# Cross-attention's query projection in seven products, with eight products of the first rows in the lead

## The chip, the cores and the metric

The kernel runs on one core of a Trainium2 chip. The metric is the device time of one execution in microseconds; the time of a kernel is the median of its runs. Engines are named as in the profile: PE is TensorE, DVE is VectorE, ACT is ScalarE, POOL is GpSimd, and SP is the engine on whose queue nearly all transfers are issued.

## What is computed

One layer of a decoder trunk in float32, with 1024 tokens and a model width of 1024. It has three sub-layers, each with an RMSNorm before and after: token mixing (attention and a state-space mixer), cross-attention into 256 memory tokens, and a gated feed-forward of hidden width 2816. The parts that matter here, with `S = D = 1024`:

```python
x = x + rms_norm(merged @ w_mix_out, g_post_mix)
h = rms_norm(x, g_pre_xa)
q = (h @ w_xq).reshape(bsz, seq, XA_HEADS, XA_HEAD_DIM)     # 4 heads of 256
...                                                         # k, v of the memory, softmax, o
x = x + rms_norm(o @ w_xo, g_post_xa)
h = rms_norm(x, g_pre_ffn)
gate, up = _split(h @ w_gu, (FFN_HIDDEN, FFN_HIDDEN))
x = x + rms_norm((silu(gate) * up) @ w_down, g_post_ffn)
```

## The kernel before

**Products.** A float32 operand is split into a rounded part `hi` (type fp32r) and a rest `lo`; a product is then three matmuls, hi·hi, hi·lo and lo·hi (`mm3`, lines 103 to 107). `hi_sb` makes the first part (line 94 on POOL, 98 on ACT) and `lo_of` the second (line 101, on DVE unless another engine is given).

**Seven products.** A 2x2 block product can be had with seven block products instead of eight (Winograd's form of Strassen's method). `winograd_weights` (line 174) forms the four combinations of weight blocks on POOL (lines 183 to 186), and splits seven blocks. `winograd_pair` (line 222) runs the seven products, 12 matmuls of 512 columns each (`acc3`, lines 211 to 218). The activation side needs seven blocks as well: `b11`, `b21`, `b22` as they are, and `t1` to `t4`, which are differences. `b11` and `b21` hold the first 512 tokens ("first rows"), the other five need the second 512 too. The feed-forward uses this form from its column block 2 on (`strassen`, line 1654, blocks 2 to 21).

**The two output projections** (`out_proj`, line 1421) go over eight chunks of 128 tokens, four for each half. A chunk multiplies 8 row blocks of a weight held in SBUF (`big_weight`, line 1352), takes the post-norm from the accumulator (square on ACT, line 1437; `rstd_of` on POOL; scaling on DVE, line 1439; addition, line 1440), stores the new x by SP's queue (line 1441), and calls `pre_norm` (line 157), which scales again (line 161), transposes eight tiles on PE (line 165) and splits them. Two accumulators (`p2`) alternate, so a chunk's matmuls wait for the scaling of the chunk before the last.

**Query projection** (lines 1501 to 1510). For each of eight column blocks `f` and each half of the tokens, `proj` (line 1466) runs 8 row blocks x 3 matmuls. Blocks 0 and 1 of the first half run under the norm of the last chunk. The other weights come by SP into the tiles `x4` and are split by `wq_load` (line 1457).

**Scores and mixing** (lines 1522 to 1570). `soft` makes the scores of a chunk for four heads in one `p2` accumulator, and the softmax; `turn_` transposes, `mix` multiplies with v. Then come `w_xo` (line 1574) and the second `out_proj`.

**Feed-forward's start** (lines 1596 to 1651). Column blocks 0 and 1 (`NSTD = 2`) are done in the standard form, four projections of 24 matmuls each for a block. Beside them `combos` (line 1631) adds hi and lo together again (`whole`, line 1624) and makes `t1`, `t3`, `t2`, and a last loop makes `t4`.

**Order and room.** The instructions of each engine are put in order ahead of time by a scheduler that runs its own timing model; `behind(marks)` ties what a block issues behind given instructions on the same engine. Tiles live in pools that open and close like stacks from the left and the right end of SBUF; a tile in a room that another tile had waits for the last use of that one. `wmix` lies in `wbigA` on the right, `w_xo` in `wbigB`; the tiles of the query and, later, of the feed-forward take the same rooms.

## Time and profile before

| | |
|---|---|
| median of 3 runs | 2554.08 us (2549.73 to 2554.72) |
| profiled execution | 2557.14 us, span 2555.3 us |
| mean granted TensorE clock | 0.994 |
| busy in the span | PE 97%, DVE 70%, ACT 44%, POOL 33% |
| PE instructions | 12378 |
| output projection and query projection | 1542 to 1728 us of the span |
| scores and mixing, second output projection | 1728 to 1885 us |
| feed-forward up to the down projection | 1885 to 2318 us |

A row of the timeline gives start, duration, engine, line and form, and in brackets the idle time just before it and what ended it. PE's durations overlap: a matmul begins before the one ahead of it has ended. A row of the stages gives for a stretch of the span each engine's busy time with its number of instructions, then the granted clock, the busy share of the transfer engines and GB/s.

### The profile page before, as it was taken

What the parts mean: (1) busy time and instruction counts of PE and PEld (TensorE: products, weight loads), DVE (VectorE), ACT (ScalarE), POOL (GpSimd) and SP (SyncE); (2) the same over time, 40 slices, a digit from 0 to 9 for tenths busy, and PEclk for the clock granted to TensorE, in tenths of its full rate; (3) what the DMA queues carried; (4) which work ended last, traced back from release to release, by engine and by line L of the source; (5) the groups of instructions that cost most, each with busy time, mean ns of one, the idle gap of its engine ahead of it and who ended that gap; (6) DMA issues with size and microseconds to landing.
All of it is one profiled execution on the core that took longest, in us unless ns stands there. A gap on an engine that the chain in (4) does not pass through costs nothing. (4 is left out here: it accounts for less than half of the span.)

```text
span 2555.3 us, 33384 instructions
## 1 busy us (share of the span) xinstructions
PE 2472.5 (97%) x12378; PEld 2030.5 (79%) x12378; DVE 1790.9 (70%) x2093; ACT 1133.7 (44%) x2023; POOL 852.2 (33%) x650
## 2 busy tenths in 40 slices
PE   7999999999999999999999999999999999999998
PEld 5788888888778778777787778887787888888877
DVE  7765877766678787698898664316458667666997
ACT  5333555555556565565554203215233333334342
POOL 3221644443211111256565140101113233223762
PEclk9999999999999999999999999999999999999999
DMA  7431443333443433365332652311231322324232
GB/s 246 157 124 58 138 133 103 107 112 109 127 108 99 114 99 99 105 209 166 106 107 61 226 194 84 116 49 34 99 123 59 95 80 75 99 84 164 99 132 99
DMA packets 255275, 293.51 MB, mean 115 GB/s; under 512 B 17023, under 2 KB 175240, under 8 KB 254986
## 3 DMA queue, kind: packets, MB, share of 16 engines
q1 hardware_dynamic: 255114, 291.40, 36.7%
q8 instruction: 97, 1.59, 0.3%
q14 instruction: 64, 0.52, 0.1%
HBM read 200.10 MB, written 74.45 MB: 107 GB/s over the span
## 5 line engine op out<-in xcount | busy, mean ns | idle before, releaser
L898 DVE TENSOR_TENSOR_SCAN n<-n,mask 128x128 f32<-128x128 f32 (+7 forms) x128 | 187.7, 1492 | 24.7 <-ACT n L897 23.4
L101 DVE TENSOR_TENSOR sw<-sf,sw 128x512 fp32r<-128x512 f32 x150 | 121.0, 819 | 82.1 <-ACT sw L98 80.6
L915 ACT ACTIVATE wth<-tr,mone 128x512 fp32r<-128x512 f32 x192 | 110.6, 585 | 83.9 <-PE tr L912 81.8
L98 ACT ACTIVATE sw<-sf 128x512 fp32r<-128x512 f32 x150 | 92.0, 626 | 112.7 <-PE mm L217 97.2
L183 POOL TENSOR_TENSOR sf<-wr,wr 128x512 f32<-128x512 f32 x38 | 58.4, 1536 | 234.0 <-DMA wr<-in_w_gu_dram 150.1
L916 DVE SCALAR_TENSOR_TENSOR wtl<-tr,wth 128x512 fp32r<-128x512 f32 x192 | 99.6, 543 | 50.8 <-ACT wth L915 50.7
L98 ACT ACTIVATE sw<-wr 128x512 fp32r<-128x512 f32 x113 | 71.2, 631 | 125.7 <-PE mm L217 124.2
L217 PE MATMUL mm<-h,sw 128*128 128x512 f32 x320 | 124.8, 391 | 1.8 <-DVE sw L101 1.8
L215 PE MATMUL mm<-h,sw 128*128 128x512 f32 x320 | 122.6, 391 | 2.9 <-ACT h L98 2.3
L216 PE MATMUL mm<-h,sw 128*128 128x512 f32 x320 | 125.1, 391 | 0.0
L101 DVE TENSOR_TENSOR sw<-wr,sw 128x512 fp32r<-128x512 f32 x113 | 108.4, 961 | 19.8 <-ACT sw L98 19.7
L680 DVE SCALAR_TENSOR_TENSOR b<-b,prmT,b 128x1023 f32<-128x1023 f32 (+2 forms) x72 | 109.6, 1522 | 16.9 <-ACT b L674 16.3
L94 POOL TENSOR_SCALAR v<-va 128x512 fp32r<-128x512 f32 x16 | 20.6, 1290 | 286.2 <-PE av L925 165.3
L897 ACT ACTIVATE n<-sc 128x512 f32<-128x512 f32 (+1 forms) x192 | 88.7, 494 | 46.8 <-PE tr L912 28.8
L152 POOL TENSOR_SCALAR rstd<-ms 128x1 f32<-128x1 f32 x74 | 29.1, 393 | 240.2 <-ACT x L1437 113.4
L104 PE MATMUL mm<-oth,bw 128*128 128x512 f32 x256 | 104.0, 406 | 2.6 <-DVE a L1237 2.3
L104 PE MATMUL p<-bw,h 128*128 128x512 f32 x256 | 99.6, 394 | 3.3 <-DVE x L1439 2.4
L105 PE MATMUL mm<-otl,bw 128*128 128x512 f32 x256 | 100.8, 394 | 0.0
L106 PE MATMUL mm<-oth,bw 128*128 128x512 f32 x256 | 100.7, 393 | 0.0
L106 PE MATMUL p<-bw,h 128*128 128x512 f32 x256 | 100.6, 394 | 0.0
L105 PE MATMUL p<-bw,h 128*128 128x512 f32 x256 | 100.5, 393 | 0.0
L912 PE MATMUL tr<-ident,n 128*128 128x128 f32 x576 | 95.2, 274 | 3.3 <-DVE wtl L916 3.3
(616 smaller groups left out, 8010.9 us busy)
## 6 DMA issues: line engine op xcount, KB each, us to landing
wr<-in_w_gu_dram SPq DMA_DIRECT2D x80, 256.0 KB
wr<-in_w_in_dram SPq DMA_DIRECT2D x36, 512.0 KB
zr<-in_w_in_dram SPq DMA_DIRECT2D x28, 512.0 KB
gu_d<-t SPq DMA_DIRECT2D x44, 256.0 KB
wraw<-in_w_in_dram SPq DMA_DIRECT2D x20, 512.0 KB
zs_d<-zo SPq DMA_DIRECT2D x32, 256.0 KB
xs_d<-b SPq DMA_DIRECT2D x32, 256.0 KB
kl<-gt SPq DMA_DIRECT2D x64, 128.0 KB
```

The source lines that it names most:

```text
L98: A.activation(o, i, AF.Copy)
L101: eng.tensor_tensor(o, i, hi.bitcast(F32), ALU.subtract)
L104: first = T.matmul(ps, sh, mh, start=start, stop=False)
L105: T.matmul(ps, sh, ml, start=False, stop=False)
L106: T.matmul(ps, sl, mh, start=False, stop=stop)
L215: T.matmul(ps, w[0][:, k, :], bh, start=first and k == 0, stop=False, skip_group_check=True)
L216: T.matmul(ps, w[0][:, k, :], bl, start=False, stop=False, skip_group_check=True)
L217: ins = T.matmul(ps, w[1][:, k, :], bh, start=False, stop=last and k == 3, skip_group_check=True)
L680: V.scalar_tensor_tensor(acc[:, sh:], y[:, :S - sh], cw(3 - sh, f), acc[:, sh:], ALU.mult, ALU.add)
L898: V.tensor_tensor_scan(nt[:, 0:L][:, ::-1], nt[:, 0:L][:, ::-1], mask[:, S - L:][:, ::-1], 1.0, ALU.mult, ALU.max)
L915: A.activation(wh[:, t0 * P:], pt[:, t0 * P:], AF.Identity, bias=mone)
L916: V.scalar_tensor_tensor(wl[:, t0 * P:], pt[:, t0 * P:], -1.0, wh[:, t0 * P:].bitcast(F32), ALU.add, ALU.subtract)
```

## The change

- The query projection is done in seven products, in two sets of four column blocks (0 to 3 and 4 to 7); a set holds two 2x2 products that share the activation blocks. So is the feed-forward from block 0 on, again with blocks 0 to 3 in two sets of two (gate and up make the 2x2). From block 4 on the feed-forward is as it was.
- In both places eight products that need only the first rows lead: with `b11` and `b21` and four weight blocks of each of two sets. Three of them have weights that are loaded under the last chunks of the output projection (`lead_weights`). Each product is issued behind the one before it (`in_turn`).
- `pre_norm` gives back its transposes as a function (`turns`); those of a chunk are issued after the next chunk's matmuls, those of the last chunk after the fourth leading product.
- `first_half` keeps an unsplit copy of the first rows (ACT), and `second_half` forms the differences from the transposes of the second rows on DVE; `other_blocks` splits `t2`, `t3`, `t4` between the later products. `combos` and `whole` are gone.
- `big_weight` takes the rooms of its eight blocks in falling order, with the raw tiles' rooms first (`wmix`) or last (`w_xo`). The query's weight quarters are loaded into the tiles of the query itself, the feed-forward's into those that its down projection uses later.
- The stores of the last two chunks are issued on ACT's queue, and the last chunk's x goes to a raw room of the weight.
- Accumulators: two banks `mm` of their own (`psa`), two `p2`, two `tr`; products also use halves of `p2`. The memory's k and v take the rooms of the unsplit copies (`xk`).

```diff
-    def pre_norm(psp, xt, yt, gbc, outs):
+    def pre_norm(psp, xt, yt, gbc, put):
         ms = mk(stats, [P, 1], F32, "ms")
         A.activation(yt, xt, AF.Square, scale=D ** -0.5, accum_out=ms)
         V.scalar_tensor_tensor(yt, xt, rstd_of(ms), gbc, ALU.mult, ALU.mult)
-        for kh, (hi, lo) in enumerate(outs):
-            pt = mk(psp, [P, 4, P], F32, "tr")
-            for k in range(4):
-                T.transpose(pt[:, k, :], yt[:, (kh * 4 + k) * P:(kh * 4 + k + 1) * P], ident)
-            A.activation(hi, pt, AF.Copy)
-            V.tensor_tensor(lo, pt, hi.bitcast(F32), ALU.subtract)
+        def turns():
+            pts = []
+            for kh in range(2):
+                pts.append(mk(psp, [P, 4, P], F32, "tr"))
+                for k in range(4):
+                    T.transpose(pts[kh][:, k, :], yt[:, (kh * 4 + k) * P:(kh * 4 + k + 1) * P], ident)
+            put(pts, yt)
+        return turns
...
-    def big_weight(wb, w, npool=0):
+    def big_weight(wb, w, npool=0, raw_on_top=False):
         wh, wl = [], []
+        def raw_room():
+            return mk(wb, [P, D], F32, "wraw", bufs=2)
+        first = [] if raw_on_top else [raw_room()]
+        rooms = {k: mk(wb, [P, 2, D], F32R, f"bw{k}", bufs=1) for k in reversed(range(KT))}
         for k in range(KT):
-            raw = mk(wb, [P, D], F32, "wraw", bufs=2)
+            raw = first.pop() if first else raw_room()
             nc.sync.dma_start(raw, w[k * P:(k + 1) * P, :])
-            both = mk(wb, [P, 2, D], F32R, f"bw{k}", bufs=1)
+            both = rooms[k]
             wh.append(both[:, 0, :])
             wl.append(both[:, 1, :])
             hi_sb(wh[k], raw, "p" if k < npool else None)
...
+            xt = mk(t4, [P, D], F32, "x4") if ci < 3 or ahead is None else ahead()
             nc.sync.dma_start(xt, x_src[c * P:(c + 1) * P, :])
...
-            order.append(nc.sync.dma_start(x_dst[c * P:(c + 1) * P, :], xt))
+            queue = nc.sync if ahead is None or ci < 2 else nc.scalar
+            order.append(queue.dma_start(x_dst[c * P:(c + 1) * P, :], xt))
             marks.append(order)
-            pre_norm(psp, xt, yt, gpre, [(hi[:, :, cs], lo[:, :, cs]) for hi, lo in nxt])
+            if late:
+                late.pop()()
+            late.append(pre_norm(psp, xt, yt, gpre, put(cs)))
...
+    def first_half(hb, xf):
+        hb["b11"], hb["b21"] = quad(accp, "a8")
+        def at(cs):
+            def put(pts, yt):
+                for nm, pt in zip(("b11", "b21"), pts):
+                    hi, lo = [t[:, :, cs] for t in hb[nm]]
+                    A.activation(hi, pt, AF.Copy)
+                    V.tensor_tensor(lo, pt, hi.bitcast(F32), ALU.subtract)
+                for x, pt in zip(xf, pts):
+                    A.activation(x[:, :, cs], pt, AF.Copy)
+            return put
+        return at
...
+    def second_half(hb, xf):
+        hb["b22"], hb["t1"] = quad(h2, "h2")
+        def at(cs):
+            def put(pts, yt):
+                b22, t1 = [[t[:, :, cs] for t in hb[nm]] for nm in ("b22", "t1")]
+                x11, x21, x2 = [x[:, :, cs] for x in xf]
+                x = yt[:, 0:HALF].rearrange("p (k t) -> p k t", t=P)
+                A.activation(b22[0], pts[1], AF.Copy)
+                V.tensor_tensor(x, pts[0], x11, ALU.subtract)
+                A.activation(t1[0], x, AF.Copy)
+                V.tensor_tensor(b22[1], pts[1], b22[0].bitcast(F32), ALU.subtract)
+                V.tensor_tensor(x2, pts[1], x, ALU.subtract)
+                V.tensor_tensor(t1[1], x, t1[0].bitcast(F32), ALU.subtract)
+                V.tensor_tensor(x11, x2, x11, ALU.subtract)
+                V.tensor_tensor(x21, x21, x2, ALU.subtract)
+            return put
+        return at
...
+    def other_blocks(hb, xf, tx):
+        hb["t2"], hb["t3"] = quad(h2, "h2")
+        hb["t4"] = tuple(mk(tx, [P, 4, HALF], F32R, "tx") for _ in range(2))
+        x3, x4, x2 = xf
+        def split(nm, x):
+            hi, lo = hb[nm]
+            for k in (0, 2):
+                hi_sb(hi[:, k:k + 2, :], x[:, k:k + 2, :], "a")
+                lo_of(lo[:, k:k + 2, :], x[:, k:k + 2, :], hi[:, k:k + 2, :])
+        return {nm: (lambda nm=nm, x=x: split(nm, x)) for nm, x in (("t2", x2), ("t3", x3), ("t4", x4))}
...
+    def split_weight(pl, tag, x, eng=V):
+        o = mk(pl, [P, 2, 4, P], F32R, tag)
+        split_ops.append([hi_sb(o[:, 0], x, "a"), lo_of(o[:, 1], x, o[:, 0], eng)])
+        return o[:, 0], o[:, 1]
+    def lead_weights(wbig, w):
+        raws = [mk(wbig, [P, 4, 2, P], F32, "wraw", 2) for _ in range(2)]
+        for kh in range(2):
+            nc.sync.dma_start(raws[kh].rearrange("p k b f -> p k (b f)"), w[kh * 512:(kh + 1) * 512, 0:2 * P].rearrange("(k p) f -> p k f", p=P))
+        ws = {(0, p): split_weight(ld, "sw", raws[0][:, :, p]) for p in range(2)}
+        o = mk(wbig, [P, 2, 4, P], F32R, "wraw", 2)
+        hi_sb(o[:, 0], raws[1][:, :, 0], "a")
+        lo_of(o[:, 1], raws[1][:, :, 0], o[:, 0])
+        ws[1, 0] = o[:, 0], o[:, 1]
+        return ws
...
+    def in_turn(ps, w, b, first, last):
+        with behind(chain[-1:]):
+            chain.append(acc3(ps, w, b, first, last))
+        return chain[-1]
+    def first_product(hb, w, nm, ps):
+        return in_turn(ps, w, hb[nm], True, nm == "b21")
+    def lead_products(hb, ws, pa, pb0):
+        first_product(hb, ws[0, 0], "b11", pa[0])
+        first_product(hb, ws[0, 1], "b11", pa[1])
+        first_product(hb, ws[1, 0], "b21", pb0)
+    def first_sum(y, pa, pb):
+        A.activation(y, pa, AF.Copy)
+        V.tensor_tensor(y, y, pb, ALU.add)
+    def other_products(hb, pa, pc, q11, q12, q21, q22, sfp, swp, y, last, blocks=None):
+        a11, a12, a21, a22 = [q[1] for q in (q11, q12, q21, q22)]
+        def combined(dst, x, z, op):
+            for o, i, j in zip(dst, x, z):
+                G.tensor_tensor(o, i, j, op)
+            return dst
+        def rooms():
+            return [mk(sfp, [P, 4, P], F32, "sf") for _ in range(2)]
+        def weights(x):
+            return [split_weight(swp, "sw", t) for t in x]
+        def products(ps, ws, nm, start, stop, then):
+            for p in range(2):
+                in_turn(ps[p], ws[p], hb[nm], start, stop)
+                then(p)
+        def block(nm):
+            if blocks is not None:
+                with behind(split_ops[-2] + split_ops[-1]):
+                    blocks[nm]()
+        with behind(rstd_ops[-1:]):
+            s1 = combined(rooms(), a21, a22, ALU.add)
+        w1 = weights(s1)
+        s2 = combined(rooms(), s1, a11, ALU.subtract)
+        s4 = combined(rooms(), a12, s2, ALU.subtract)
+        s3 = combined(a21, a11, a21, ALU.subtract)
+        products(pc, w1, "t1", True, False, lambda p: A.activation(y[p][1][1], pc[p], AF.Copy))
+        block("t2")
+        w2 = weights(s2)
+        products(pa, w2, "t2", False, False, lambda p: A.activation(y[p][0][1], pa[p], AF.Copy))
+        block("t3")
+        w3 = weights(s3)
+        products(pa, w3, "t3", False, False, lambda p: V.tensor_tensor(y[p][1][1], y[p][1][1], pa[p], ALU.add))
+        w4 = weights(s4)
+        products(pc, w4, "b22", False, True, lambda p: V.tensor_tensor(y[p][0][1], y[p][0][1], pc[p], ALU.add))
+        block("t4")
+        w7 = weights(a22)
+        products(pa, w7, "t4", False, True, lambda p: last(p, pa[p]))
...
+        def lead_xq():
+            with behind(marks[AFTER_M]):
+                lead.update(lead_weights(wbig, a["w_xq"][0]))
+            return mk(wbig, [P, D], F32, "wraw", 2)
+        lead = {}
+        out_proj(1, mg[1], wmix, t4, psp, x_in, x2_d, gpost, gpre, second_half(hx, xf), lead_xq)
...
+    xa, xb, xc = (bank(), bank()), two_banks(), two_banks()
+    lead_products(hx, lead, xa, xb[0])
...
+            n11, n12 = quarter(qT[6]), quarter(qT[7])
+            q21, q22, q12 = [parted(*r) for r in ((halves_of(4)[1], halves_of(5)[1]), (halves_of(2)[0], halves_of(3)[0]), (halves_of(0)[1], halves_of(1)[1]))]
+            for q, kh, c0 in ((n11, 0, 4), (n12, 1, 4), (q21, 0, 2), (q22, 1, 2), (q12, 1, 0)):
+                done = quarter_load(q, w_xq, kh, c0 * P)
+            n0, n1, q1 = [split_weight(swp, "sw", x, e) for x, e in ((n11[1][0], G), (n11[1][1], V), (q12[1][1], V))]
+            with behind([first_product(hx, n0, "b11", xc[0])] + split_ops[-1]):
+                late.pop()()
+            def more(kh, c0):
+                q = quarter(mk(t4, [P, S], F32, "x4"))
+                quarter_load(q, w_xq, kh, c0 * P)
+                return q
+            first_sum(halves_of(0)[0], xa[0], xb[0])
+            with behind([done]):
+                q11 = more(0, 0)
+            first_product(hx, n1, "b11", xc[1])
+            first_product(hx, q1, "b21", xb[1])
+            first_sum(halves_of(1)[0], xa[1], xb[1])
+            for p in range(2):
+                first_product(hx, split_weight(swp, "sw", n12[1][p]), "b21", xb[p])
+                first_sum(halves_of(4 + p)[0], xc[p], xb[p])
+            other_products(hx, xa, xb, q11, q12, q21, q22, sfp, swp, rows_of(0), lambda p, ps: fourth(2 + p, ps), other_blocks(hx, xf, tx))
+            n21, n22 = more(0, 6), more(1, 6)
+            other_products(hx, xc, xb, n11, n12, n21, n22, sfp, swp, rows_of(4), lambda p, ps: fourth(6 + p, ps))
...
-        for f in range(KT):
-            w = wqs[f] if f < 2 else wq_load(t4, "x4", colblock(a["w_xq"][0], f * P))
-            for half in range(2):
-                if f < 2 and half == 0:
-                    continue
-                pq = proj(w, hx[half])
-                A.activation(qT[f][:, half * HALF:(half + 1) * HALF], pq, AF.Copy)
...
-        wxo = big_weight(wbig, a["w_xo"][0], 2)
+        wxo = big_weight(wbig, a["w_xo"][0], 2, True)
...
-        def whole(pair, k, eng):
-            t = mk(t2, [P, HALF], F32, "t2")
-            eng.tensor_tensor(t, pair[0][:, k, :].bitcast(F32), pair[1][:, k, :].bitcast(F32), ALU.add)
-            return t
-        def split(t, pair, k):
-            hi_sb(pair[0][:, k, :], t, "a")
-            lo_of(pair[1][:, k, :], t, pair[0][:, k, :])
-        def combos(k):
-            x11, x12, x22 = [whole(b, k, V) for b in (b11, b12, b22)]
-            V.tensor_tensor(x11, x12, x11, ALU.subtract)
-            split(x11, t1, k)
-            V.tensor_tensor(x12, x22, x12, ALU.subtract)
-            split(x12, t3, k)
-            V.tensor_tensor(x22, x22, x11, ALU.subtract)
-            split(x22, t2_, k)
...
+        n11, n12, q11, n21 = [quarter(t[:, i]) for t in (fg, fw) for i in range(2)]
+        quarter_load(n11, w_gu, 0, 2 * P)
+        q12 = fmore(1, 0)
+        quarter_load(n12, w_gu, 1, 2 * P)
+        q21, q22 = fmore(0, FFN), fmore(1, FFN)
+        quarter_load(q11, w_gu, 0, 0)
+        quarter_load(n21, w_gu, 0, FFN + 2 * P)
+        y = [results() for _ in range(2)]
+        q1, n0, n1 = [split_weight(swp, "sw", x, e) for x, e in ((q12[1][1], G), (n11[1][0], V), (n11[1][1], V))]
+        first_sum(y[0][0][0], fa[0], fb[0])
+        with behind([first_product(hw, q1, "b21", fb[1])] + split_ops[-1]):
+            late.pop()()
...
+        first_product(hw, n0, "b11", fc[0])
+        first_product(hw, n1, "b11", fc[1])
+        t = mk(ld, [P, 2, HALF], F32, "sw")
+        yn = [[[t[:, p], None], [None, None]] for p in range(2)]
+        for p in range(2):
+            first_product(hw, split_weight(swp, "sw", n12[1][p]), "b21", fb[p])
+            first_sum(yn[p][0][0], fc[p], fb[p])
...
+        other_products(hw, fa, fe, q11, q12, q21, q22, sfp, swp, y, both_gated(y, 0, "xk0"), other_blocks(hw, xf, tx))
+        n22 = fmore(1, FFN + 2 * P)
+        for r in yn:
+            r[0][1], r[1][1] = [mk(t2, [P, HALF], F32, "t2") for _ in range(2)]
+        other_products(hw, fc, fe, n11, n12, n21, n22, sfp, swp, yn, both_gated(yn, 2, "xk1"))
```

More of the change, by code (lines that the diff above doesn't have):

```diff
@@ L189, in winograd_weights @@
         for i in ((6, 0, 1, 2, 3, 4, 5) if pool_ops else range(7)):
-            both[i] = mk(swp, [P, 2, 4, P], F32R, "sw")
+            both[i] = mk(firstp if firstp is not None and i in (0, 3) else swp, [P, 2, 4, P], F32R, "sw")
         for i, t in enumerate((a11, s1, s2, a12, s3, s4, a22)):
@@ L220, in hybrid_block, with winograd_pair @@
     ends, held, held_taps = [], [], []
-    def winograd_pair(psp, ws, hb, y, between=None):
+    def winograd_pair(psp, ws, hb, y, between=None, banks=None):
         wa11, ws1, ws2, wa12, ws3, ws4, wa22 = ws
-        pa_, pc_ = mk(psp, [P, HALF], F32, "mm"), mk(psp, [P, HALF], F32, "mm")
+        pa_, pc_ = banks[:2] if banks is not None else [mk(psp, [P, HALF], F32, "mm") for _ in range(2)]
         acc3(pa_, wa11, hb["b11"], True, False)
@@ L241, in winograd_pair @@
         if between is None:
-            pb_ = mk(psp, [P, HALF], F32, "mm")
+            pb_ = banks[2] if banks is not None else mk(psp, [P, HALF], F32, "mm")
             acc3(pb_, wa12, hb["b21"], True, True)
@@ L1419, in hybrid_block, with out_proj @@
     marks = []
-    def out_proj(half, act, w, t4, psp, x_src, x_dst, gpost, gpre, nxt):
+    late = []
+    def out_proj(half, act, w, t4, psp, x_src, x_dst, gpost, gpre, put, ahead=None):
         wh, wl = w
@@ new lines, in hybrid_block, with both_gated, end @@
+        xt4.close()
+        tx = pool(q4, "tx", 2, side="right")
+        fc, fb, fe = [(fbank(), fbank()) for _ in range(3)]
+        first_product(hw, n0, "b11", fc[0])
[5 more added lines that the diff above has]
+            first_sum(yn[p][0][0], fc[p], fb[p])
+        def both_gated(y, f0, rooms):
+            sgs = []
+            def end(p, ps):
+                if not sgs:
+                    t = mk(xk, [P, 4, HALF], F32, rooms)
+                    sgs.extend(t[:, i] for i in range(4))
+                gated(f0 + p, 0, y[p][0][0], ps, sgs[2 * p])
+                gated(f0 + p, 1, y[p][0][1], y[p][1][1], sgs[2 * p + 1])
+            return end
```

163 lines of the change are left out of this document (84 added, 79 removed).

## The prediction

> **What bounds the kernel now.** I read the page first, then busy time by stage, then TensorE's idle gaps in the order of time.
>
> ```profile
> span 2555.3 us, 33384 instructions
> PE 2472.5 (97%) x12378; PEld 2030.5 (79%) x12378; DVE 1790.9 (70%) x2093; ACT 1133.7 (44%) x2023; POOL 852.2 (33%) x650
> ```
>
> TensorE is busy for nearly the whole span. An average does not say which stage is bound by it, so here are the stages that the diff touches: the query projection (1636 to 1728), scores and mixing (1728 to 1788), the first standard block of the feed-forward (1885 to 1932), its change to seven products (1932 to 1951), and the steady rest.
>
> ```profile
> core 0: us, PE busy (x) PEld busy (x) DVE busy (x) ACT busy (x) POOL busy (x), PEclk, DMA share, GB/s
> 1636.00:1728.00 92.00, 92.00 (x416) 76.46 (x416) 15.36 (x15) 16.93 (x28) 5.79 (x8) 1.00 0.22 69
> 1728.00:1788.00 60.00, 55.17 (x268) 45.65 (x267) 41.77 (x64) 32.09 (x95) 8.68 (x5) 0.97 0.11 36
> 1885.00:1932.00 47.00, 46.53 (x212) 38.27 (x211) 36.11 (x41) 15.90 (x26) 16.25 (x13) 1.00 0.28 86
> 1932.00:1951.00 19.00, 13.30 (x55) 9.79 (x54) 19.00 (x33) 7.65 (x14) 1.42 (x1) 1.00 0.18 60
> 1951.00:2318.00 367.00, 367.00 (x1614) 303.63 (x1612) 236.49 (x275) 134.48 (x232) 115.39 (x72) 1.00 0.27 82
> ```
>
> The query projection is pure TensorE time: 92.00 of 92 us, VectorE at 15.36. Here a matmul less is time less. From 1932 to 1951 it is the reverse: VectorE has no free moment and TensorE waits. Steady seven-product work (last row) keeps TensorE full with VectorE at 236.49 of 367. TensorE's gaps, from its timeline (start, duration, and in brackets the idle time before and who ended it):
>
> ```profile
> 1732.14 3.72 PE L1529 MATMUL p<-kT,qT 128*128 128x256 f32 x16 [1.23 <-ACT prob L1533]
> 1744.25 3.72 PE L1529 MATMUL p<-kT,qT 128*128 128x256 f32 x16 [0.81 <-ACT prob L1533]
> 1898.27 0.51 PE L104 MATMUL mm<-h,qhi 128*128 128x512 f32 x1 [0.25 <-ACT h L166]
> 1899.00 0.51 PE L105 MATMUL mm<-h,qhi 128*128 128x512 f32 x1 [0.22 <-DVE h L167]
> 1938.79 0.50 PE L215 MATMUL mm<-h,sw 128*128 128x512 f32 x1 [2.31 <-ACT h L98]
> 1944.74 0.50 PE L217 MATMUL mm<-a,sw 128*128 128x512 f32 x1 [1.58 <-DVE sw L101]
> 1949.56 0.50 PE L217 MATMUL mm<-h,sw 128*128 128x512 f32 x1 [1.80 <-DVE sw L101]
> ```
>
> The feed-forward's entry loses 0.25 + 0.22 + 2.31 + 1.58 + 1.80 = 6.2 us, nearly all of it while VectorE makes the combined blocks of the activations.
>
> **Term 1, matmuls that go.** The price of one is its distance to the next in an unbroken stream, not its duration of 0.39 us, since they overlap:
>
> ```profile
> 1621.79 0.39 PE L104 MATMUL p<-bw,h 128*128 128x512 f32 x1
> 1623.15 0.39 PE L104 MATMUL p<-bw,h 128*128 128x512 f32 x1
> ```
>
> Six steps lie between these two: 1.36 / 6 = 0.227 us. Query projection before: 8 column blocks x 2 halves x 8 row blocks x 3 = 384 matmuls. After: 4 pairs of blocks x 7 products x 12 = 336. So 48 go. In the feed-forward only blocks 0 and 1 change: 2 x 4 x 24 = 192 become 2 x 7 x 12 = 168, so 24 go. 72 x 0.227 = **16.3 us**. The Trainium skill (TensorE: Matmul & The Clock Gate, "Back-to-back issue gap") gives about 131 ns for each 512-column matmul in a sustained stream; by it the term would be 72 x 0.131 = 9.4 us, an estimate from that page. The two rows above contradict it here.
>
> **Term 2, the feed-forward's entry.** The changed kernel no longer rebuilds x from hi + lo (five additions for each of four k). It forms the differences in `second_half`, straight from the transposes, chunk by chunk under the output projection. At most the 6.2 us go. What replaces them is the same engine's work in both entries, so I count it. A product of 12 takes 2.72 us. Eight lead (21.8), ten follow in the first `other_products` (27.2), two rounds of transposes take 1.7: TensorE has 50.7 us in an entry. VectorE's prices:
>
> ```profile
> L101 DVE TENSOR_TENSOR qlo<-x,qhi x8: 1225/1226/1226, 1658.1 to 1727.5; 128x1024 fp32r<-128x1024 f32 x8
> L101 DVE TENSOR_TENSOR sw<-wr,sw x5: 679/681/1780, 1891.1 to 1952.4; 128x512 fp32r<-128x512 f32 x5
> L101 DVE TENSOR_TENSOR qlo<-wr,qhi x2: 1219/1774/2328, 1905.9 to 1911.2; 128x1024 fp32r<-128x1024 f32 x2
> L183 POOL TENSOR_TENSOR sf<-wr,wr x18: 1287/1295/5892, 1949.6 to 2274.8; 128x512 f32<-128x512 f32 x18
> L244 DVE TENSOR_TENSOR t<-t,mm 128x512 f32<-128x512 f32 x19 | 13.0, 686 | 9.2 <-PE mm L217 9.1
> ```
>
> (min/median/max in ns; the last row has the mean.) Chunk 7's own norm takes 3.8 us (rows below). The six VectorE operations of `second_half` for chunks 6 and 7: 12 x 0.69 = 8.2. Four lead splits 2.7, four first sums 2.7, ten weight splits 6.8, six block splits 6 x 1.23 = 7.4, four additions 2.7. Sum 34.3 of 50.7 us. An operation that meets a GpSimd one is 1.1 us longer (681 against 1780, 1226 against 2328). GpSimd has about nine beside it (eight combinations, one split), four more if the second set's start early: 13 x 1.1 = 14.3, together 48.6. It still fits, but the last few splits may be late. The Trainium skill (SBUF — State Buffer, "Who interferes with whom") says that a VectorE operation with two SBUF inputs and a GpSimd one that reads SBUF exclude each other for a whole instruction. That rule speaks against this change, which puts both engines' work in one place; the +1.1 us agrees with it.
>
> Bounds for what is lost in an entry: 0, as in the steady stretch, and 5.7, as in 1932 to 1951. I take 1.5 us for each of the two, since 34 to 49 of 51 us is nearer to the steady row's load.
>
> **Chunk 7's norm under the lead products.**
>
> ```profile
> 1635.12 1.03 ACT L1437 ACTIVATE x<-p 128x1024 f32<-128x1024 f32 x1 [3.27 <-PE p L106]
> 1637.24 1.28 DVE L1439 SCALAR_TENSOR_TENSOR x<-p,rstd,g_post_mix 128x1024 f32<-128x1024 f32 x1 [3.10 <-POOL rstd L153]
> 1638.56 1.23 DVE L1440 TENSOR_TENSOR x<-x,x 128x1024 f32<-128x1024 f32 x1
> 1641.97 1.29 DVE L161 SCALAR_TENSOR_TENSOR x<-x,rstd,g_pre_xa 128x1024 f32<-128x1024 f32 x1 [0.99 <-POOL rstd L153]
> ```
>
> From the last matmul's end to the operand of the transposes: 1643.3 − 1635.1 = 8.2 us. The new order puts them behind four products (10.9 us), so they cost no wait; with only the three `lead` products in front (8.2 us) there would be no slack. The first needs of chunk 7's columns come after all eight (t1), about 23.6 us in; they are ready near 18 (transposes at 12, the queued lead split at 14, 4.1 us of `second_half`). Stores of chunks 6 and 7 move from SP's queue to ScalarE's. Behind the store there waits only the Square that needs the same sum: the price is the issue, 0.33 us by SP's row, under TensorE; I take 0.
>
> ```profile
> 1639.81 0.33 SPq L1441 DMA_DIRECT2D x_d<-x  x1
> 1460.00:1470.00 10.00, 10.00 (x46) 8.09 (x45) 7.00 (x7) 2.23 (x3) 6.30 (x5) 1.00 1.05 377
> 1457.46 7.36 DMA wraw<-in_w_mix_out_dram
> 1468.40 5.02 DMA wraw<-in_w_mix_out_dram
> ```
>
> The lead's further weights come by SP into rooms that the output projection's weights leave. With the falling order, as I read the pools, the first quarters lie over block 0, 1, 2, free from about 9 us before the last matmul. Five loads of 512 KB at the 377 GB/s of that stretch take 7 us, at half of it 14, so all are in between −2 and +5 us; the fourth product starts at +8.2. Cost 0; what it costs without this cover is the second rival.
>
> **Scores and the next weights.** Before, parts of the first scores ran between projection products; now chunk 0's last head needs the very last product and its eviction.
>
> ```profile
> 1657.22 0.60 ACT L1510 ACTIVATE qT<-mm 128x512 f32<-128x512 f32 x1 [7.94 <-PE mm L106]
> 1735.92 3.62 PE L1529 MATMUL p<-kT,qT 128*128 128x256 f32 x16
> 1755.76 43.51 SPq L1356 DMA_DIRECT2D wraw<-in_w_xo_dram  x8
> 1805.07 1.23 DVE L101 TENSOR_TENSOR bw<-wraw,bw 128x1024 fp32r<-128x1024 f32 x1 [1.87 <-ACT bw L98]
> ```
>
> Bounds: −2.0 (the two gaps above go) and +3.6 (a chunk's scores with nothing beside them). I take +1.0, near the 0.60 of the eviction. The raw rooms of `w_xo` now lie over the last query blocks, not the first, so the loads start up to one chunk of scores (3.6 us) later than 1755.8. Before, the last split ended at 1806.3 and still fed TensorE without a gap. Bounds 0 and 3.6; I take 0.5.
>
> **Sum:** −16.3 − 6.2 + 1.5 + 1.5 + 1.0 + 0.5 = −18.0 us. Against the profiled execution (2557.1 us, 1.8 us over its span, 3.1 over the median) that is 2539.1; against the median, 2554.1 − 18.0 = **2536.0**.
>
> **Rivals.** *VectorE takes back half.* Both entries lose 5.7 us like 1932 to 1951, scores 1.0, `w_xo` 0.5: −22.5 + 12.9 = −9.6, 2544.5. For it: the fixed chain of products lets TensorE do nothing else while it waits, and 48.6 of 50.7 is tight. Against: 34.3 without collisions, and the steady row.
>
> *Weights late behind a fixed order: slower.* If rooms come free only at chunk 7's end and SP moves one load at a time at 7.36 us, the query's sixth product (the fifth load) waits from about 14.5 to 36.8 + 1.3 = 38.1, 23.6 us. In the feed-forward the fourth product needs the second load (16.0 against 8.2: 7.8), and the first combination needs the fifth load (9.3 more). 40.7 − 22.5 = +18, 2572. It decides above 22.5 us of such waits; at the 5.02 us of the other row the same count gives about 17, and the change would still win by 5. Against: rooms free early, 377 GB/s with loads in flight together.
>
> *It doesn't save what it says.* The products fall in number but gaps everywhere (5.7 twice, 3.6, 3.6) eat all but 3.9 us: 2550.2, within what can be told from no change.
>
> **How the numbers follow.** 0.2% is 5.1 us, about what a measurement of this kernel can tell from no change. Forecast 0.67; half taken back 0.16; slower 0.11; nothing saved 0.06. Faster: 0.67 + 0.16 = 0.83. Low: all stalls gone, 16.3 + 6.2 + 2.0 = 24.5, 2529.6, rounded to 2529. High: 2550, which takes in the first and third rivals and all upper bounds together; outside are the slower case and the rare better one.
>
> **What would show it.** TensorE's 512-column matmuls fall by 72. The gaps at the feed-forward's entry are under 2 us together. Transposes of chunk 7 follow the fourth lead product with no idle time. Scores start within 1 us after the last product. I am wrong if TensorE waits for a load or a lead split between the products, if VectorE is full in an entry and TensorE is not, or if `w_xo` splits hold the second output projection.

## The result: slower by 0.56%

| | before | after |
|---|---|---|
| median (runs) | 2552.72 us (2549.73 to 2554.72, 4) | 2567.87 us (2562.7 to 2568.16, 4) |
| ratio to before, 95% interval | 1 | 1.0056 [1.0038, 1.0073] |
| profiled execution: time, span | 2557.14, 2555.3 us | 2562.7, 2561.0 us |
| query: first product to last | 91.7 us | 106.3 us |
| TensorE idle at the feed-forward's entry | 6.2 us | 8.8 us |

The forecast was 2536.0 us with a range up to 2550; the time is above both, on the side that had a chance of 0.11. The two profiled executions lie 5.6 us apart, the two medians 15.2: that of before is over its median and that of after under it. So the stages below tell where the time goes, and the medians how much.

The page of the changed kernel:

```profile
span 2561.0 us, 33402 instructions
PE 2460.5 (96%) x12306; PEld 2017.4 (79%) x12306; DVE 1818.6 (71%) x2131; ACT 1164.5 (45%) x2075; POOL 884.7 (35%) x672
```

TensorE has 72 matmuls fewer (12378 to 12306), as forecast, and 12 us less to do, and the span is longer all the same. By stage (the query, scores and mixing, the feed-forward's entry, its steady rest):

```profile
core 0: us, PE busy (x) PEld busy (x) DVE busy (x) ACT busy (x) POOL busy (x), PEclk, DMA share, GB/s
1634.00:1741.00 107.00, 89.09 (x369) 69.70 (x367) 56.70 (x60) 34.10 (x56) 31.74 (x22) 0.94 0.19 63
1741.00:1800.00 59.00, 55.67 (x275) 46.07 (x275) 40.72 (x63) 32.31 (x96) 9.87 (x5) 1.00 0.17 54
1897.00:1960.00 63.00, 54.19 (x234) 43.70 (x233) 55.39 (x59) 31.18 (x51) 33.30 (x23) 0.95 0.23 76
1960.00:2330.00 370.00, 369.45 (x1630) 305.59 (x1629) 228.34 (x268) 134.12 (x229) 107.71 (x70) 1.00 0.27 84
```

The query was 92.00 us of TensorE in 92; now it is 89.09 in 107, and the granted clock is 0.94. Scores and mixing, and the steady seven-product work, are as before. What TensorE waited for in the query (engine, line, awaited: us in total, times, longest):

```profile
PE p L220 <- DVE qT L1579: 11.8, 2, 7.7
PE p L220 <- DVE qT L1620: 1.6, 2, 0.8
PE p L220 <- ACT qT L1612: 1.4, 2, 0.7
PE p L220 <- ACT qT L1615: 1.4, 2, 0.7
PE p L220 <- ACT sw L98: 0.9, 1, 0.9
PE p L220 <- DVE qT L1618: 0.8, 1, 0.8
```

The two long waits and one of the short ones in TensorE's timeline:

```profile
1660.85 0.76 PE L220 MATMUL p<-a,sw 128*128 128x512 f32 x1 [7.74 <-DVE qT L1579]
1669.84 0.76 PE L220 MATMUL p<-a,sw 128*128 128x512 f32 x1 [4.03 <-DVE qT L1579]
1719.23 0.50 PE L220 MATMUL p<-h,sw 128*128 128x512 f32 x1 [0.69 <-ACT qT L1615]
```

Two kinds. Two long waits for a `first_sum` (L1579), 11.8 us together; and short ones: seven of 0.69 to 0.78 us and one of 0.87 us for a split. Six of the seven stand before the second product of a pair, for the evacuation (L1612, L1615) or addition (L1618, L1620) of the first. The seventh, at 1719.23, stands before the first product of a pair: it waits for the evacuation of the product just ahead, which lies in the other half of its tile. No load is in the list. The 106.3 us are about: 336 matmuls x 0.227 = 76.3; chunk 6's and 7's transposes 1.6; 12 matmuls of the first scores that run between the last two products 2.6; idle time 17.9; about 5 more for two products at half clock (below); and the rest, about 3, for some ten restarts, 0.3 each.

The feed-forward's entry, from TensorE's timeline:

```profile
1908.41 0.50 PE L222 MATMUL p<-a,sw 128*128 128x512 f32 x1 [0.64 <-POOL sw L101]
1916.37 0.77 PE L220 MATMUL mm<-a,sw 128*128 128x512 f32 x1 [4.52 <-DVE t L1579]
1943.22 0.50 PE L220 MATMUL mm<-h,sw 128*128 128x512 f32 x1 [2.60 <-ACT t L1615]
```

With the 1.05 us for a lead split before them, 8.8 us. The longest is again a wait for a first sum, and the product behind it ran slowly: from 1916.37 to 1921.55, 5.18 us, with a granted clock of 0.52 over the first 5 us.

**Why the sum was late.** VectorE's timeline in the query, from the sixth product's run to the eighth's, and GpSimd's beside it:

```profile
1649.16 2.88 DVE L101 TENSOR_TENSOR sw<-qT,sw 128x512 fp32r<-128x512 f32 x2
1651.96 3.44 DVE L101 TENSOR_TENSOR sw<-sf,sw 128x512 fp32r<-128x512 f32 x2
1655.33 0.68 DVE L1505 TENSOR_TENSOR h<-tr,h 128x512 fp32r<-128x512 f32 x1
1655.93 0.67 DVE L1506 TENSOR_TENSOR xk<-tr,x 128x512 f32<-128x512 f32 x1
1656.52 1.78 DVE L1507 TENSOR_TENSOR h<-x,h 128x512 fp32r<-128x512 f32 x1
1658.22 0.68 DVE L101 TENSOR_TENSOR sw<-sf,sw 128x512 fp32r<-128x512 f32 x1
1658.83 0.68 DVE L1508 TENSOR_TENSOR xk<-xk,xk 128x512 f32<-128x512 f32 x1
1659.43 0.68 DVE L1509 TENSOR_TENSOR xk<-xk,xk 128x512 f32<-128x512 f32 x1
1660.03 0.67 DVE L1579 TENSOR_TENSOR qT<-qT,p 128x512 f32<-128x512 f32 x1
...
1664.59 4.50 DVE L101 TENSOR_TENSOR h<-xk,h 128x1024 fp32r<-128x1024 f32 x2
1669.02 0.68 DVE L1579 TENSOR_TENSOR qT<-qT,p 128x512 f32<-128x512 f32 x1
...
1648.05 3.44 POOL L1587 TENSOR_TENSOR sf<-sf,x 128x512 f32<-128x512 f32 x2
1651.45 3.40 POOL L1587 TENSOR_TENSOR qT<-x,qT 128x512 f32<-128x512 f32 x2
1654.82 2.93 POOL L1587 TENSOR_TENSOR sf<-qT,sf 128x512 f32<-128x512 f32 x2
```

The sixth product ended at 1653.11 and its sum could have run then. It ran at 1660.03, since the splits of w1, chunk 7's operations and a split of s2 stood before it in VectorE's queue, none of them needed yet. From 1653.10 to 1669.80 VectorE is busy without a pause (16.70 us), and TensorE for 4.96 us. The pairs of splits at 1649.16 and 1651.96 took 2.88 and 3.44 us, beside GpSimd's combinations; without them a pair takes 1.28 (the row at 1648.30 of the last kernel below).

This gives three suspects: the order of VectorE's queue, the halves of a two-bank tile (`two_banks`) as one room, and GpSimd's combinations.

### The profile page after: what moved, and what is told of

It reads as the page before. It is cut to its first block, busy times and chain, and to the rows that moved or that the text cites. A ratio compares the mean times of both kernels' runs of the same rounds, so it can differ in the third digit from the quotient of the medians.

```text
span 2561.0 us, 33402 instructions
## 1 busy us (share of the span) xinstructions
PE 2460.5 (96%) x12306; PEld 2017.4 (79%) x12306; DVE 1818.6 (71%) x2131; ACT 1164.5 (45%) x2075; POOL 884.7 (35%) x672
## 5 line engine op out<-in xcount | busy, mean ns | idle before, releaser
L101 DVE TENSOR_TENSOR sw<-sf,sw 128x512 fp32r<-128x512 f32 x166 | 137.3, 837 | 91.0 <-ACT sw L98 88.8
L98 ACT ACTIVATE sw<-sf 128x512 fp32r<-128x512 f32 x166 | 102.6, 627 | 136.3 <-PE mm L222 112.2
L220 PE MATMUL mm<-h,sw 128*128 128x512 f32 x368 | 143.3, 389 | 2.6 <-ACT t L1615 2.6
L221 PE MATMUL mm<-h,sw 128*128 128x512 f32 x368 | 143.2, 389 | 0.0
L222 PE MATMUL mm<-h,sw 128*128 128x512 f32 x368 | 140.9, 389 | 0.0
L921 DVE SCALAR_TENSOR_TENSOR wtl<-tr,wth 128x512 fp32r<-128x512 f32 x192 | 99.5, 543 | 48.2 <-ACT wth L920 48.2
L188 POOL TENSOR_TENSOR sf<-wr,wr 128x512 f32<-128x512 f32 x36 | 51.0, 1416 | 205.3 <-DMA wr<-in_w_gu_dram 140.6
```

Of the source, the lines that this page charges most:

```text
L98: return A.activation(o, i, AF.Copy)
L101: return eng.tensor_tensor(o, i, hi.bitcast(F32), ALU.subtract)
L220: T.matmul(ps, w[0][:, k, :], bh, start=first and k == 0, stop=False, skip_group_check=True)
L221: T.matmul(ps, w[0][:, k, :], bl, start=False, stop=False, skip_group_check=True)
L222: ins = T.matmul(ps, w[1][:, k, :], bh, start=False, stop=last and k == 3, skip_group_check=True)
L921: V.scalar_tensor_tensor(wl[:, t0 * P:], pt[:, t0 * P:], -1.0, wh[:, t0 * P:].bitcast(F32), ALU.add, ALU.subtract)
```

## The experiments

Each kernel is compared with the kernel before on the same chip.

**The feed-forward half alone.** The query projection as before the change, the rest as after (the old `wq_load` and `proj` come back for the query).

> The query projection is as before the change (standard form, 384 matmuls, plain splits after the transposes); the feed-forward's start, the rooms in falling order and the later transposes are as in the change. Theory A (the loss sits in the query projection's seven products): that stage is back at about 91.7 us, the feed-forward keeps its gain of about 6 us, the whole is about 2546 us (2542 to 2549), faster than before. Theory B (the loss sits in what both places share, the output projections with later transposes, or the rooms): it stays above 2553 us.

2553.6 us, ratio 0.9998 [0.9989, 1.0006]. The feed-forward half is worth nothing; so, if the two halves add up, the whole loss, some 15 us, is the query's. Theory A had the place right and the time wrong, as the feed-forward keeps no gain (its entry has 9.1 us of idle time). The time is theory B's, but not its cause: from first to last matmul the two output projections take 92.7 and 96.9 us before, and 93.4 and 96.9 here.

**Single banks.** The four accumulators `xb`, `xc` of the query as tiles of one bank each; for that the pool is opened anew, and chunk 7's transposes get a pool beside it.

```diff
-    xa, xb, xc = (bank(), bank()), two_banks(), two_banks()
+    psq = pool(psq_, "psq", 4, PSUM)
+    xb, xc = [tuple(mk(psq, [P, HALF], F32, "mm") for _ in range(2)) for _ in range(2)]
```

> The change, with the query's four shared accumulator halves as four tiles of one bank each (pool opened over the same banks); nothing else. Theory A1 (a product waits for the reading of the other half of its two-bank tile): the eight gaps of 0.7 to 0.9 us between the later products go (about 7.6 us with their restarts), the seventh product no longer waits 7.7 us for a sum on VectorE, the eighth waits for the first pair's second sum, 3 to 5 us: 2548 to 2554 us. Theory A2 (VectorE's backlog alone, the tile plays no part): all gaps stay, 2565 to 2569 us.

2554.49 us, 0.9999 [0.9988, 1.001]: the loss is gone, half a microsecond outside theory A1's range. The query takes 90.5 us instead of 106.3; 2.4 us of that difference are the 12 matmuls of the scores, which here run after the query's last product. All the short waits have left the timeline. In the query remain:

```profile
1658.94 0.76 PE L220 MATMUL mm<-a,sw 128*128 128x512 f32 x1 [5.08 <-DVE qT L1579]
1669.54 0.79 PE L220 MATMUL mm<-h,sw 128*128 128x512 f32 x1 [3.05 <-DVE qT L1579]
```

The seventh product (column 4 into `xb[0]`) no longer waits at all. In the change it waited 7.74 us for the sum that reads `xb[1]`, which it does not touch. A half of a tile stands for the whole tile in the order of reads and writes.

**No combinations.** GpSimd's combinations of the query's first set are left out (the weights go in uncombined), two-bank tiles as in the change.

> The change, with GpSimd's eight combinations of the query's first set left out (plain weight quarters take their place in the products). Theory A2 (GpSimd's run of combinations stretches VectorE's operations, and the sums come late): VectorE's operations between 1643 and 1658 us take about 7 us less, the seventh product waits under 2 us instead of 7.7, the eighth under 2 instead of 4, 2551 to 2556 us; the gaps of 0.7 to 0.9 us stay. Theory A1 alone (the place in VectorE's queue, not its speed): the seventh product still waits over 5 us, 2562 to 2567 us.

2561.68 us, 1.0032 [1.0017, 1.0047], which neither theory alone gives. The seventh product's wait fell from 7.74 to 1.60 us; the eighth's rose from 4.03 to 5.99:

```profile
1656.65 0.47 PE L220 MATMUL p<-a,sw 128*128 128x512 f32 x1 [1.60 <-DVE qT L1579]
1665.61 0.76 PE L220 MATMUL p<-a,sw 128*128 128x512 f32 x1 [5.99 <-DVE qT L1579]
```

The combinations make the first wait, but taking them away gives back 6 us of 15, not the whole.

**Other banks in the feed-forward.** The names `fb` and `fc` of its accumulators change places.

> The change, with the feed-forward's fifth and sixth products put into the banks of the last chunk's accumulator and the seventh and eighth into those of the fourth product, the reverse of the change. If the fifth product waits for its banks (released by a sum on VectorE), its 4.5 us go and nothing comes in their place: 4 to 7 us less than the change, 2561 to 2564 us. If it waits for a weight split or for VectorE as such, the wait moves to the next product and the time stays at 2567 to 2569 us.

2567.77 us, 1.0047 [1.0033, 1.006], as expected if the banks play no part, and the 4.5 us wait stands as it was:

```profile
1913.82 0.63 PE L220 MATMUL mm<-a,sw 128*128 128x512 f32 x1 [4.51 <-DVE t L1579]
```

Which bank the fifth product gets is not its cause.

**Sums first.** On single banks, the same work in another order: chunk 7's last four VectorE operations stand behind the first sum of column 4, w2's splits and the first block's behind the sum of column 5, the feed-forward's n12 splits behind its second first sum, and the second set's sigmoids behind the first set's evacuations.

```diff
-                V.tensor_tensor(b22[1], pts[1], b22[0].bitcast(F32), ALU.subtract)
...
+                if p == 0:
+                    with behind(s_4):
+                        rest()
...
+            with behind([s_1]):
+                wn = split_weight(swp, "sw", n12[1][p])
```

> The four accumulators of the projection in single banks, and VectorE's queue in another order: in the projection the last norm's lo and sum operations and the combined weights' splits stand behind the first sums; in the feed-forward the splits of n12 stand behind the second first-sum, and the second set's sigmoids behind the first set's evacuations of t2. The same work. Against the kernel with single banks alone (2554.5 us; waits of 5.08 and 3.05 us in the projection, 4.50 and 3.22 us in the feed-forward, all behind a first sum or an evacuation). Theory Q, the place in the queue: the 5.08 falls under 1.5, the 3.05 under 1, the 4.50 to about 1.5, the 3.22 under 0.5; some 11 us and the half clock behind them go: 2539 to 2545 us. Theory L, VectorE's load (too much work in the entry, GpSimd's collisions with it): the waits only move to the next product; over 2550 us. Theory B, the bank of the changed accumulators in the feed-forward: the 4.50 stays.

2540.67 us, 0.9948 [0.9935, 0.9962]: faster than both kernels, with nothing taken out. The query takes 82.5 us. What remains of its waits, and of the feed-forward's:

```profile
1656.34 0.47 PE L220 MATMUL mm<-a,sw 128*128 128x512 f32 x1 [2.04 <-DVE qT L1589]
1887.33 0.47 PE L220 MATMUL p<-a,sw 128*128 128x512 f32 x1 [2.03 <-ACT sw L98]
1900.02 0.77 PE L220 MATMUL mm<-a,sw 128*128 128x512 f32 x1 [3.55 <-DVE xk L1511]
```

The total is inside the expectation of theory Q; two single waits are not. The 5.08 was to fall under 1.5 and is 2.04. The 4.50 is gone from the fifth feed-forward product, but a new 3.55 stands at the sixth, which waits for L1511's read of chunk 7's transposes; that read now comes after the second first sum, among splits of weights. The waits of 3.05 and 3.22 us are gone.

**Sums first, two banks.** The same order with the change's tiles.

> Sums first as in the 2540.7 us kernel, but the projection's accumulators stay halves of two-bank tiles. Theory B (a product in one half waits for the read of the other): the eight waits of 0.7 to 0.9 us before every second product stay, and the wait at the sums is longer: 2549 to 2555 us, 9 to 14 slower. If the tiles don't matter once the sums are early, within 2 us of 2540.7.

2559.26 us, 1.002 [1.0011, 1.0028], 18 us above the same order on single banks, more than the 9 to 14 expected. The query takes 102.3 us, again with the 12 score matmuls in it. Its long waits, and one of the six of 0.69 to 0.78 us that are left:

```profile
1656.28 0.47 PE L220 MATMUL p<-a,sw 128*128 128x512 f32 x1 [4.70 <-DVE qT L1589]
1690.05 0.50 PE L220 MATMUL p<-h,sw 128*128 128x512 f32 x1 [4.13 <-DVE qT L1633]
1703.52 0.50 PE L220 MATMUL p<-h,sw 128*128 128x512 f32 x1 [0.69 <-ACT qT L1624]
```

So the tiles are the larger of the two causes in the query, and an early sum does not help a product that waits for its neighbour's.

**The feed-forward half, sums first.** The query as before the change, the feed-forward with its sums first; here w1's splits also stand behind L1511, and both sets' sigmoids behind the first set's evacuations.

> The query projection as before the change, the feed-forward as in the change, with its first sums first and the sigmoids behind the evacuations (no combination held). The feed-forward half alone in the change's order took 2553.6 us with 9.1 us of idle time in the entry. By the forecast's terms the feed-forward's share is 24 x 0.227 = 5.4 us of products and up to 6.2 us of idle time: with 2 to 5 us of idle time left, 2546 to 2550 us. If the entry is bound by VectorE's load and not by order, 2553.

2545.07 us, 0.9961 [0.9948, 0.9974], about 10 us faster than before and 1 us under the expected range, where the half in the change's order was worth 0. Idle time in the entry is 1.31 + 0.62 + 1.71 = 3.6 us instead of 9.1.

**Held combinations.** On single banks, in VectorE's old order (but for one split of s2, which now follows the sums): GpSimd reads one column of a first sum, and its combinations (the query's s2, s4, s3; all in the feed-forward) come behind that copy.

```diff
+        def hold(x):
+            t = mk(stats, [P, 1], F32, "hold", 1)
+            return G.tensor_scalar(t, x[:, 0:1], 1.0, None, ALU.mult)
...
+        with behind(held_by):
+            s2 = combined(rooms(), s1, a11, ALU.subtract)
```

> The accumulators in single banks, VectorE's order as in the change. GpSimd's second to fourth combinations in the projection, and all four in the feed-forward, start only when the second first-sum is done (a one-column copy on GpSimd reads it). The same work, later. Theory Q: the sums still stand behind the splits in the queue, but the operations before them are shorter (0.64 instead of 1.7 us each): the 5.08 falls to about 2.5, the 4.50 to about 2; 2548 to 2551 us. Theory L with the collisions as the main part: both fall under 1 us; 2543 to 2546 us. If neither matters, 2554.

2578.83 us, 1.0095 [1.0082, 1.0109]: far outside every theory. Its first query product came at 1648.2 us, 14 us late, in code that the edit does not touch. I ran it again without the new tile: the copy takes a column of the pool's tag `ms`.

> The held combinations alone again, on single banks. The first try had one more small tile, and its first product of the projection came 14 us later than in the kernel without it, so its time said nothing on the combinations; now the held copy takes a column of a pool that was there. If that was the only disturbance, the projection starts at 1632 to 1639 us as in the other kernels. In the first try's trace the waits of 5.08 and 4.50 us were gone but 10.2 us stood at a late evacuation in the feed-forward. Theory L (GpSimd's collisions stretch VectorE's work): projection without waits, total 2545 to 2550 us with the new wait of about 10. Theory Q alone: 2554 or over.

2546.02 us, 0.9966 [0.9955, 0.9977], inside theory L's range. The query starts at 1634.9 and takes 81.5 us, with waits of 1.28, 0.45 and 0.64 us. So on single banks, keeping the combinations out of the way mends the query as well as the order does (82.5). The feed-forward then has one long wait, for an evacuation that stands late in ScalarE's queue:

```profile
1923.88 0.80 PE L220 MATMUL mm<-h,sw 128*128 128x512 f32 x1 [10.84 <-ACT t L1626]
```

**Both.** Sums first and combinations held, first with the extra tile, on single banks and on two:

> Both edits together, on single banks. Theory Q: all four waits under 1 us; the projection from its first to its last product in 79 to 82 us (before 91.7, the change 106.3) and the feed-forward's entry with under 3 us of idle time: 2536 to 2541 us, the forecast's place, faster than both kernels. Theory L: new waits at the t2 and t3 products, since the combinations then run beside the splits of the blocks: 2545 to 2550 us.

> Both edits, but the accumulators in halves of two-bank tiles as in the change. If the two halves of a tile are one room for the order of reads and writes, the eight waits of 0.7 to 0.9 us before every second product stay, and so does about half of the kernel's loss: 2547 to 2555 us. If the short waits were only what the late sums left behind, the time is that of the single banks within 1 us.

2568.93 us (1.0056 [1.0043, 1.0068]) and 2583.25 us (1.0111 [1.0094, 1.0128]). Both carry the late start, so their totals say nothing against before. Against each other, two banks cost 14.3 us here too, of which up to 4.0 may lie ahead of the query (it starts at 1646.2 and at 1650.2); the short waits are in the second one's timeline. Then without the tile, and with the two further orders of the feed-forward:

> Single banks, the sums first, and the combinations held, without the extra tile; in the feed-forward the combined weights' splits also stand behind the last read of the transposes' banks and the first set's sigmoids behind its own evacuations of t2. Waits left in both entries together under 4 us (sums first alone: 2.0 and 6.2). If collisions matter beside the order: 2534 to 2538 us, below sums first (2540.7). If only the order matters: 2539 to 2542.

2538.17 us, 0.9938 [0.9925, 0.9951], the fastest kernel of this study: 2.5 us under sums first, which the intervals do not tell apart, so whether holding the combinations adds to the order stays open. The query takes 81.8 us. Its stages, in the same division as for the change:

```profile
1632.00:1714.00 82.00, 79.50 (x356) 64.69 (x355) 57.05 (x60) 33.13 (x55) 32.15 (x23) 1.00 0.25 82
1714.00:1773.00 59.00, 53.90 (x258) 44.89 (x257) 38.99 (x57) 29.26 (x90) 9.85 (x5) 0.94 0.16 54
1876.00:1939.00 63.00, 59.85 (x265) 47.68 (x264) 59.55 (x63) 32.28 (x55) 35.41 (x25) 1.00 0.28 94
```

TensorE is busy for 79.50 of the query's 82 us, with the same 57 us of VectorE and 32 of GpSimd as in the change. VectorE around the second first sum:

```profile
1648.30 1.28 DVE L101 TENSOR_TENSOR sw<-sf,sw 128x512 fp32r<-128x512 f32 x2
1651.08 0.69 DVE L1590 TENSOR_TENSOR qT<-qT,mm 128x512 f32<-128x512 f32 x1 [0.90 <-PE mm L222]
1653.80 0.69 DVE L1590 TENSOR_TENSOR qT<-qT,mm 128x512 f32<-128x512 f32 x1 [2.03 <-PE mm L222]
```

Now VectorE waits for the product, 0.90 and 2.03 us, and not the product for VectorE.

## Why the prediction was wrong

**Term 1 was right**: 72 matmuls fewer, and TensorE has 12 us less to do. In the query's own time its 48 show in part. From 91.7 to 81.8 us is 9.9, but before the change 13 matmuls of the scores (about 2.8 us) ran between the query's products and now run after them. So some 7 us of the 10.9 are left; against them stand waits of 2.4 us (1.68, 0.56 and 0.17) and the restarts behind them. From the query's first product to the second output projection's first matmul it is 153.6 us before, 165.7 in the change, 156.5 on single banks, 148.2 with sums first, 144.2 with held combinations and 147.4 with both.

**The step that failed is the bound for what is lost in an entry**, "I take 1.5 us for each of the two, since 34 to 49 of 51 us is nearer to the steady row's load". Its upper bound was 5.7; the query lost 24 us (106.3, where 91.7 − 10.9 + 1.5 = 82.3 was meant). It failed in two ways.

*The accumulators were not looked at.* The prediction counts no wait between a product and the reader of the tile that it writes. `two_banks` stands in the diff: two products write the halves of one tile, and each waits until the other half has been read. That cost 13 to 15 us by the single-bank kernel (2567.87 to 2554.49, or 1.0056 to 0.9999 of before): in the query, which went from 106.3 to 90.5 with 2.4 us of it only moved, seven short waits and the seventh product's long one, with their restarts and the half clock behind them. Neither a rival nor the "what would show it" list had it.

*VectorE was summed over the entry, not followed in its queue.* The sum itself holds: in the first 50.7 us of the fast kernel's query VectorE is busy for 45.0, between the 34.3 and 48.6 of the prediction, and TensorE for 48.2. But in the change VectorE was full from 1653.10 to 1669.80 while TensorE was not, one of the signs that the prediction named for being wrong. What decides is which operation stands before the one that TensorE awaits: 7 us of work without a due time stood before a 0.7 us sum. Order alone brought the query from 90.5 to 82.5 us. The rival "VectorE takes back half" had the right engine and the wrong price: its 5.7 us an entry is a mean over a stretch in which TensorE had other work.

**Collisions**: the price of 1.1 us was about right (a pair of splits 2.88 and 3.44 instead of 1.28, so 0.8 and 1.1 for one), but I spread thirteen of them over 50 us. GpSimd's first eight combinations run without a pause from 1644.1 to 1657.8, just ahead of the seventh product. Held back, they brought single banks from 0.9999 to 0.9966 of before. That is the place where the rule of the Trainium skill (SBUF — State Buffer, "Who interferes with whom"), that a VectorE operation with two SBUF inputs and a GpSimd read exclude each other, had its weight; the trace agrees with it: beside GpSimd, L1505 with one input in an accumulator took 0.68 us and L1507 with both in SBUF 1.78. A chance of its own would have been the better use of it.

**Term 2 was wrong as the change stands**: the 6.2 us went, and 8.8 came. With sums first the feed-forward half gave −10 us, and the forecast's share for it was −5.4 − 6.2 + 1.5 = −10.1. In the change, the sum at 4.52 us and an evacuation at 2.60 us, both queued behind work not yet due, took it all: 2.6 us more idle time than before, and the slow product behind the first.

**Chunk 7's norm** was hidden as forecast: its transposes follow the fourth product without a gap (1646.62, that product's end 1646.78). **The loads** came in time; no wait for one is in the list above, so the rival "weights late", whose time of 2572 is near the result, is not what happened, and that nearness is chance. The sign that TensorE would wait for a lead split did show, but only with 1.05 + 0.64 us in the feed-forward and 0.17 in the query. **Scores** were to cost +1.0 between −2.0 and +3.6: 12 of their matmuls ran between the query's last products, two followed at once and the next after a gap of 0.25 us, and the stage took 59.6 us instead of 62.0, a little below the lower bound. `w_xo` held nothing, and the second output projection took 96.9 us in both. The range's lower half was within reach of the idea: 2538.17 us, −15.8 us by its ratio of 0.9938 against −18.0.

## What to carry to other kernels

Before a chain of products in a fixed order is priced, list for each product the last reader of the room that it overwrites, and what stands ahead of that reader on its engine: an engine at half load over a stage still delays it by whatever was queued first. Give independent accumulators tiles of their own, since two halves of one tile share their waits. Where a short operation lets TensorE go on, set it ahead of longer work that is due later, and start another engine's bulk work only after it.

## What the runs showed of the hardware

**The clock after a stall.** Beside the waits stands a second price. Windows of the changed kernel, before the two long waits, behind the first and behind the second (the figure after the busy times is the granted clock):

```profile
1640.00:1653.00 13.00, 12.83 (x60) 10.13 (x58) 12.96 (x13) 8.86 (x17) 11.36 (x8) 1.00 0.51 161
1660.80:1665.80 5.00, 4.95 (x12) 3.64 (x12) 5.00 (x4) 0.74 (x1) 3.87 (x3) 0.57 0.67 231
1669.80:1674.80 5.00, 4.96 (x12) 3.79 (x12) 2.19 (x2) 0.00 (x0) 1.87 (x2) 0.50 0.18 48
```

Twelve matmuls take 4.95 us and then 5.45 us (1669.84 to 1675.29) instead of 2.72, about 5 us more. In the traces of this study the waits of 3 us or more in these two entries were followed by a clock of 0.50 to 0.71 over the next 5 us. Of those between 2.0 and 2.9 us some were (2.04 and 2.62: 0.66) and some were not (2.60, 2.75 and 2.90: 1.00). After 1.68 and 1.71 us it was 1.00, but three times a shorter one was followed by a lower clock: 1.22 us with one of 0.63 close behind it by 0.73, the like in two more kernels by 0.70 and 0.68, while the same two waits in other kernels (1.31 and 0.62) left it at 1.00. So no length of wait separates the two here. The Trainium skill (TensorE: Matmul & The Clock Gate, "Part 1: The HAM clock gate (the "warmup" mystery)") tells of a window of about 3.4 us that runs freely, an idle one bringing half clock. That it runs freely would fit that equal waits end differently; that it takes an idle window of 3.4 us the measurement does not bear out, since waits of 2.04 us and less had it too.

**One small tile.** A new tile of 128 x 1 floats in the pool `stats` made the time up to the query 13.3 us longer in one pair of kernels that differ there in nothing else (1648.2 against 1634.9) and 13.8 in the other (1646.15 against 1632.31), though the second pair's feed-forward orders differ too. In the profiles of the first pair the same matmuls are 2.6 us late by 87 us of the span, 10.5 by 609 us and 11.0 at the first output projection's start. What the tile moved, and why that costs, was not tried and stays open.
